# A hybrid encoder step on one core: key tiles of full height for the delta-rule state, one decay buffer, and closer transfers in the build-time plan

## The chip, the cores and the metric

The kernel runs on one core of a Trainium2 chip. A core has a matrix engine (TensorE, PE in the profile; PEld is its weight load), three elementwise engines (VectorE = DVE, ScalarE = ACT, GpSimd = POOL) and SyncE (SP), which issues nearly all transfers here. The engines run beside each other, each in the order of its own instruction list, and wait for each other by semaphores. Matmuls read SBUF and write PSUM, which has eight banks. The metric is device time of the core in microseconds; less is better.

## The reference, cut to what matters

Two layers over 2048 prompt frames and 32 frames of a running stream, width 1024, in float32. Layer 0 is sliding-window attention, layer 1 gated DeltaNet with 8 heads of 128 keys by 128 values, in chunks of 64 frames. Each layer has an input projection, a gate, an output projection and a residual add; RMSNorm stands ahead of each layer and at the end. The change concerns the delta rule, per head and chunk:

```
v_new = u - w @ s
o = (q * exp(g)) @ s + intra @ v_new
s = s * exp(g_last) + (k * exp(g_last - g)).T @ v_new
```

Here `u` and `w` come out of a triangular system in the chunk's keys, `s` is the 128x128 state of the head, and `intra` is the masked product of queries and keys times a decay.

## The kernel before, in words

The frames are cut into four slabs of 512 (the second carries the 32 sample frames too, 544 columns). All of layer 0 goes over the slabs, then all of layer 1. A projection is a run of blocks: 128 output features, 8 slices of the contraction, three matmuls each (the operands are split into a high and a low part in a faster float format), so 24 matmuls of 512 columns or 48 of 272 per block. In between, side work runs as generators: attention in layer 0, convolution and delta rule in layer 1.

In layer 1 the heads go in pairs: head x = 0 of a pair lives on partitions 0 to 63 (64 frames), head x = 1 on 64 to 127. Four chunks of a pair of heads are a *quad*, two quads a *pair* of a slab; with the sample's lone quad there are 33 quads, 132 chunks. Per quad, `local_quad` (line 1491) turns the keys from columns to frames through PSUM into `kd` (line 1507, 128 partitions by 4 chunks by 128), loads the decay table `e` (line 1502, two buffers), makes it an exponential, scales it, multiplies it with the products of keys and queries into `md`, `mo` and `it`, and scales `kd` (line 1546). `inverse` (line 1562) solves the triangular systems of both quads of a pair on VectorE, in some 62 dependent small steps with the tiles `tl` and `sub`, then transposes into `tq` (line 1597) and finishes with 32x32 matmuls. `chain_quad` (line 1635) goes through the chunks in order: state times keys and queries (`tb<-st,kq`), `r` on VectorE, the solve (`tb<-r,btt`; in the last pair the tile is called `kqs`), a copy `vn` on ScalarE, then the state's update and the output matmul (`tb<-vn,bit`), and on VectorE two state additions (`st`) and the output `o`. The update takes the two heads as two matmuls over 64 partitions each, into two PSUM tiles (`p3`, tag `tc`, and `p2`, tag `tb`). `p2` also holds the output matmul's result:

```
up = [p3[:, 0:P], p2[:, 2 * P : 3 * P]]
...
    self.mm(up[x], q["kd"][rows, c, :], vn[rows], True, True)
self.mm(p2[:, P : 2 * P], q["it"][:, c, :], vn, True, True)
```

A float32 matmul of the program shows as two passes in the profile.

The order on each engine is made at build time. Every operation is recorded with a cost (`Estimate`), and `Order.flush` (line 313) replays them as a list scheduler: on each engine the operation that can start first goes next; among those ready, the lowest rank, where an evacuation of a projection (`EVAC`) and the steps of the chain (`CHAIN`) are moved ahead. An operation on a PSUM bank waits for all earlier ones of other engines in that bank. Transfers are one queue in this plan: a transfer starts at the later of 1500 ns after its issue and the end of the one before it, lasts its bytes / 250 ns (line 150), and has landed 500 ns after that. Up to 25 us of plan time its length is taken times `CLOSE` = 0.7 (line 341). The plan has 216 ns for a projection matmul of 512 columns. The hardware keeps the order, not the times.

In layer 0, `out_blocks` (line 881) makes the output projection: each block loads the residual into `xr`, VectorE adds the product onto it (the evacuation), and the sum goes to memory. Weights arrive as `wr` and are split: ScalarE rounds to `wh` (high), VectorE subtracts to another `wh` (low); six `wh` buffers go round. Beside this, `keep_ahead` (line 425) loads the weights of layer 1, splits them and stores both parts, three transfers of 256 KB per half block.

Of the kernel before, what the change touches and what calls it, by code (L numbers as in the profile page):

```python
# [13 lines left out]
AF = mybir.ActivationFunctionType  # L14
ALU = mybir.AluOpType

P = 128
# [5 lines left out]
CH = 64  # L23
# [188 lines left out]
class Order:  # L212
# [2 lines left out]

    ENGINES = ("tensor", "vector", "scalar", "gpsimd", "sync")

    START, EARLY, CLOSE = 25000, 5000, 0.7

    EVAC, CHAIN = 400, 600  # L220
# [92 lines left out]
    def flush(self):  # L313

        overs = []
        for p in self.places.values():
            if p.old and p.over is None:
                p.over = Op(None)
                overs.append(p.over)
                for o in p.old.ops:  # L320
                    self.link(o, p.over)
                for o in {id(o): o for o in p.ops}.values():
                    self.link(p.over, o)
                    if o.gang:
                        self.link(p.over, o.gang)
        self.wait = {e: [] for e in self.ENGINES}
        ready = {e: [] for e in self.ENGINES}
        for o in [o for o in overs + self.ops if o.left == 0]:
            self.settle(o)
        while any(self.wait.values()) or any(ready.values()):  # L330
            when = {e: max(self.free[e], 0.0 if ready[e] else self.wait[e][0][0]) for e in self.ENGINES if ready[e] or self.wait[e]}
            e = min(when, key=when.get)
            now = when[e]
            while self.wait[e] and self.wait[e][0][0] <= now:
                _, rank, o = heapq.heappop(self.wait[e])
                heapq.heappush(ready[e], (rank, o))
            _, op = heapq.heappop(ready[e])
            op.call()
            if op.dma:
                self.free[e] = now + 60  # L340
                self.dma = max(now + 1500, self.dma) + op.cost * (self.CLOSE if now < self.START else 1)
                op.ends = {"dma": self.dma + 500}
            else:
                self.free[e] = now + op.cost
                op.ends = {e: self.free[e]}
            op.start = now
            self.finish(op)
        assert all(o.done for o in self.ops)
        self.ops = []
# [49 lines left out]
class Kern:  # L399
# [848 lines left out]
    def delta_setup(self, bp):  # L1248
        nc = self.nc
        self.bp = bp  # L1250
        one = lambda shape, tag, dt=F32: self.t(bp, shape, tag, dt, bufs=1)
        self.st = one([P, DNH, P], "st")
        self.hist = one([P, 24, 3], "hist")
        nc.gpsimd.memset(self.hist, 0.0)
        self.hsmp = one([P, 24, 3], "hsmp")
        nc.sync.dma_start(self.hsmp, self.io["cv"])
        self.csmp = one([P, 24, 3], "csmp")

        self.cw = one([P, 96], "cw")
        nc.vector.tensor_scalar(out=self.cw, in0=self.par[:, PC_CW : PC_CW + 96], scalar1=0.5, scalar2=None, op0=ALU.mult)  # L1260
        self.dg = one([P, 1], "dgn")
        nc.vector.tensor_scalar(out=self.dg, in0=self.par[:, PC_DG : PC_DG + 1], scalar1=0.5, scalar2=None, op0=ALU.mult)
        self.na_ = one([P, 4], "na")
        nc.scalar.activation(self.na_, self.par[:, PC_AL : PC_AL + 4], AF.Exp)
        nc.vector.tensor_scalar(out=self.na_, in0=self.na_, scalar1=-1.0, scalar2=None, op0=ALU.mult)

        self.tts = [one([P, 4, P], f"btt{i}") for i in range(2)]
        self.its = [one([P, 4, P], f"bit{i}") for i in range(4)]

        def zeros():  # L1270
            for x in (*self.its, *self.tts, self.st):
                nc.gpsimd.memset(x, 0.0)
                yield 1000

        self.spawn(zeros(), "zeros", 5000)
        self.npair = self.nconv = 0
        self.chained, self.order, self.quads, self.had = set(), [], [], [None, None]
# [213 lines left out]
    def local_quad(self, q, tab, off, md, mo, c0):  # L1491

        nc, bp, m = self.nc, self.bp, 4
# [5 lines left out]
        half = [slice(x * CH, (x + 1) * CH) for x in range(2)]  # L1499
        kq = q["kq"]  # L1500
        yield kq
        e = self.t(bp, [P, m, CH], "e", bufs=2)
        for x in range(2):
            src = tab["gcd"][x, off : off + m].rearrange("c t -> (c t)").unsqueeze(0).broadcast_to([CH, m * CH])
            nc.sync.dma_start(e[x * CH : (x + 1) * CH].rearrange("p c t -> p (c t)"), src)
        sx, ss = [self.t(bp, [P, 2, 4], k, bufs=b) for k, b in (("sx", 2), ("ss", 6))]
        kd = self.t(bp, [P, m, P], "kd", bufs=4)
        q["kd"] = kd
        for x, rows in enumerate(half):
            pk = yield from self.bank("ta")  # L1510
            for c in range(m):
                self.tp(pk[:, c * P : (c + 1) * P], kq[:, c, x, :])
            yield
            nc.scalar.copy(kd[rows].rearrange("p c d -> p (c d)"), pk[rows, : m * P])
            for c in range(m):
                junk = pk[:, c * P : (c + 1) * P]
                nc.scalar.activation(junk, junk, AF.Square, accum_out=sx[:, x, c : c + 1])
            self.give("ta")
            yield 0
# [20 lines left out]
        kds, ri, nbk = small("kds"), small("ri"), small("nbk")  # L1540
# [2 lines left out]
        nc.vector.scalar_tensor_tensor(out=nbk[:, :m], in0=ri[:, :m], scalar=-1.0, in1=tsl("egc"), op0=ALU.mult, op1=ALU.mult)  # L1543
        q["ri"], q["nbk"] = ri, nbk
        for c in range(m):
            nc.scalar.activation(kd[:, c, :], kd[:, c, :], AF.Copy, scale=kds[:, c : c + 1])
        yield e
        g = pg[:, : m * P].rearrange("p (c t) -> p c t", c=m)
        for x in range(2):
            rows = slice(x * CH, (x + 1) * CH)  # L1550
# [11 lines left out]
    def inverse(self, quads, md, mo):  # L1562


        nc, bp = self.nc, self.bp
        m = 4 * len(quads)
        cg, nj = 32 // m, m
# [26 lines left out]
            if j % 3 == 2:  # L1594
                yield

        tq = self.t(bp, [P, 8, 32], "tq", bufs=1)[:, :nj]
        nc.vector.transpose(out=tq, in_=t3.rearrange("p i j -> p j i"))
        tc_ = tq.rearrange("p j (g c) -> p c (j g)", g=cg)
        tr = self.t(bp, [P, 8, 32], "trc", bufs=1)[:, :m]  # L1600
# [34 lines left out]
    def chain_quad(self, q, tab, off, states, gated, put):  # L1635


        nc, bp, m = self.nc, self.bp, 4
        tt = nc.vector.tensor_tensor
        kq = q["kq"]  # L1640
# [5 lines left out]
        for c in range(m):  # L1646
            state = yield from states(c)
            p1 = yield from self.bank("tb")
            self.issue.lead = Order.CHAIN
            for x in range(2):  # L1650
                self.mm(p1[:, x * P : (x + 1) * P], kq[:, c, x, :], state[:, x, :], True, True)
            r = self.t(bp, [P, P], f"r{q['i']}", bufs=1)
            qs = self.t(bp, [P, P], f"qs{q['i']}", bufs=1)
            half = [slice(y * CH, (y + 1) * CH) for y in range(2)]
            for x, rows in enumerate(half):
                nc.vector.scalar_tensor_tensor(
                    out=r[rows], in0=p1[rows, x * P : (x + 1) * P], scalar=q["nbk"][rows, c : c + 1], in1=q["vb"][rows, c, :],
                    op0=ALU.mult, op1=ALU.add)
            for x, rows in enumerate(half[::-1]):
                nc.scalar.activation(  # L1660
                    qs[rows], p1[rows, x * P : (x + 1) * P], AF.Identity, scale=tab["egq"][rows, off + c : off + c + 1])
            self.give("tb")
            self.issue.lead = 0
            yield
            p2 = yield from self.bank("tb")
            self.issue.lead = Order.CHAIN
            self.mm(p2[:, 0:P], q["tt"][:, c, :], r, True, True)
            vn = self.t(bp, [P, P], f"vn{q['i']}", bufs=1)
            nc.scalar.copy(vn, p2[:, 0:P])
            self.issue.lead = 0  # L1670
            yield

            p3 = yield from self.bank("tc")
            up = [p3[:, 0:P], p2[:, 2 * P : 3 * P]]
            self.issue.lead = Order.CHAIN
            for x in range(2):
                rows = slice(x * CH, (x + 1) * CH)
                self.mm(up[x], q["kd"][rows, c, :], vn[rows], True, True)
            self.mm(p2[:, P : 2 * P], q["it"][:, c, :], vn, True, True)
            for x in range(2):  # L1680
                nc.vector.scalar_tensor_tensor(
                    out=state[:, x, :], in0=state[:, x, :], scalar=tab["egl"][:, x, off + c : off + c + 1],
                    in1=up[x], op0=ALU.mult, op1=ALU.add)
            tt(out=o[:, c, :], in0=p2[:, P : 2 * P], in1=qs, op=ALU.add)
            self.issue.lead = 0
            self.give("tb")
            self.give("tc")
            yield
            nc.scalar.activation(qs, o[:, c, :], AF.Square, accum_out=so[:, c : c + 1])
            states.done(c)  # L1690
# [562 lines left out]
```

## Time and profile before

| what | before |
|---|---|
| time, median of 3 runs | 2347.42 us (2346.01 to 2352.44) |
| profiled execution | 2349.7 us, of it span 2347.9 us |
| PE busy | 2243.8 us (96%), 14759 matmuls |
| DVE busy | 1724.0 us (73%) |
| ACT busy | 1262.7 us (54%) |
| POOL busy | 467.8 us (20%) |
| DMA | 382.75 MB, mean 163 GB/s |
| mean granted TensorE clock | 0.980 of full speed |

The span runs from the first to the last instruction; the time has a little around it. Busy is the union of an engine's instructions. Matmuls overlap each other in the records, so the distance from start to start tells what one costs in a row, not its length. Layer 1 begins at about 1000 us. All compute instructions carry the same source line (that of a recording helper), so groups are told apart by their tiles: `tc<-vn,kd` writes tile `tc` from `vn` and `kd`.

### The profile page before, as it was taken

To read this page: it belongs to the slowest core of one execution; us is meant where nothing else is said; L and a number is where in the kernel's file an instruction comes from. 1 tells how busy PE (TensorE), PEld (TensorE's weight loads), DVE (VectorE), ACT (ScalarE), POOL (GpSimd) and SP (SyncE) were. 2 spreads that over 40 slices of the span, in tenths; PEclk is the share of its full clock that TensorE was granted. 3 is DMA by queue.
4 is the path that set the end of the run, shared out by engine and by line. 5 is a ranking of instruction groups with operands and counts; after the bars stand their busy time and mean duration, and the time that the engine had idled before them with its cause. 6 is when DMAs were issued, how large, how long until landed. Compare 5 with 4: busy or idle time off the path is not lost.

```text
span 2347.9 us, 44428 instructions
## 1 busy us (share of the span) xinstructions
PE 2243.8 (96%) x14759; PEld 1842.6 (78%) x14759; DVE 1724.0 (73%) x5330; ACT 1262.7 (54%) x3792; POOL 467.8 (20%) x738
## 2 busy tenths in 40 slices
PE   8999999989999999999999999989999999999997
PEld 6777899877777777777788788867798777777776
DVE  7785667757665565688987677888886888786876
ACT  6664566546554553556566355465644465535533
POOL 0120000301110001222233031231313222122222
PEclk9999999999999999999999999999999999999998
DMA  8567655765443226544533673433457634476442
GB/s 272 190 203 231 219 187 183 222 220 193 153 138 112 66 64 203 180 133 127 173 95 112 207 240 102 133 115 125 149 177 226 188 117 137 139 225 206 153 139 68
DMA packets 222832, 382.75 MB, mean 163 GB/s; under 512 B 29922, under 2 KB 45194, under 8 KB 222602
## 3 DMA queue, kind: packets, MB, share of 16 engines
q1 hardware_dynamic: 220154, 377.75, 50.4%
q8 instruction: 116, 1.90, 0.3%
q10 hardware_dynamic: 2448, 2.16, 0.3%
q14 instruction: 114, 0.93, 0.1%
HBM read 311.63 MB, written 68.19 MB: 162 GB/s over the span
## 4 chain that ended last, share of the span: by engine, by line
PE 66%; DVE 22%; ACT 6%; issue 3%; DMA 1%; POOL 1%; SPq 0%; DVEq 0%; ACTq 0%; POOLq 0%
PE pj L185 47%; PE tb L185 7%; PE ta L185 6%; PE tc L185 4%; DVE cy L185 4%; DVE sub L185 3%; DVE tl L185 3%; ACT ta L185 2%; DVE ml L185 1%; DVE md L185 1%; DVE r L185 1%; PE ms L185 1%; ACT kd L185 1%; DVE st L185 1%; DVE kq L185 1%
## 5 line engine op out<-in xcount | busy, mean ns | idle before, releaser
L185 PE MATMUL pj<-hk,wh 128*128 128x512 f32 (+1 forms) x8184 | 1770.5, 363 | 34.0 <-DVE xr L185 16.3
L185 PEld LDWEIGHTS pj<-hk,wh 128*128 128x128 f32 x8184 | 1326.5, 191 | 246.4 <-issue 29.2
L185 DVE SCALAR_TENSOR_TENSOR cy<-cx,cw,cy 128x512 f32<-128x512 f32 x360 | 230.5, 651 | 45.7 <-ACT cy L185 40.9
L185 DVE TENSOR_TENSOR wh<-wr,wh 128x512 fp32r<-128x512 f32 x224 | 159.1, 712 | 139.5 <-ACT wh L185 129.4
L185 ACT CAST wh<-wr 128x512 fp32r<-128x512 f32 x224 | 138.0, 618 | 203.2 <-PE pj L185 174.0
L185 ACT ACTIVATE qs<-tb,egq 64x128 f32<-64x128 f32 x264 | 95.7, 362 | 90.5 <-DVE r L185 79.6
L185 POOL TENSOR_TENSOR hk<-of,hk 128x256 fp32r<-128x256 f32 (+1 forms) x72 | 53.4, 742 | 444.8 <-ACT hk L185 439.2
L185 ACT ACTIVATE s<-s,mx 128x256 f32<-128x256 f32 (+1 forms) x272 | 132.0, 487 | 7.5 <-DVE mx L185 7.2
L185 DVE TENSOR_TENSOR sub<-ml,tl 128x60 f32<-128x60 f32 (+24 forms) x527 | 125.8, 239 | 10.2
L185 ACT ACTIVATE cx<-cy 128x512 f32<-128x512 f32 (+1 forms) x96 | 61.1, 636 | 130.4 <-DVE cy L185 95.7
L185 DVE TENSOR_TENSOR tl<-tl,sub 128x60 f32<-128x60 f32 (+24 forms) x527 | 123.0, 233 | 10.1
L185 DVE CUSTOM_DVE_ANT_0 s<-ta,bias 128x256 f32<-128x256 f32 (+1 forms) x272 | 96.2, 404 | 25.6 <-PE ta L185 25.5
L185 DVE SCALAR_TENSOR_TENSOR r<-tb,nbk,vb 64x128 f32<-64x128 f32 x264 | 91.7, 348 | 29.8 <-PE tb L185 25.3
L185 ACT ACTIVATE qs<-o 128x128 f32<-128x128 f32 x132 | 40.7, 308 | 132.2 <-DVE o L185 126.8
L185 ACT COPY cx<-pj 128x512 f32<-128x512 f32 (+2 forms) x149 | 64.1, 445 | 77.8 <-PE pj L185 66.0
L185 PE MATMUL tb<-st,kq 128*128 128x128 f32 x512 | 95.0, 287 | 5.5 <-DVE st L185 5.0
L185 PEld LDWEIGHTS tb<-st,kq 128*128 128x128 f32 x512 | 82.7, 194 | 20.4 <-DVE st L185 12.3
L185 DVE SCALAR_TENSOR_TENSOR st<-st,egl,tc 128x128 f32<-128x128 f32 x128 | 44.3, 346 | 59.4 <-PE tc L185 56.9
L185 ACT COPY pt<-tb 128x512 f32<-128x512 f32 (+2 forms) x144 | 70.6, 528 | 26.4 <-PE tb L185 26.1
L185 DVE TENSOR_SCALAR s<-s,den 128x256 f32<-128x256 f32 (+1 forms) x272 | 81.7, 352 | 1.1
L185 PE MATMUL tc<-pt,vt 128*64 128x128 f32 (+2 forms) x1056 | 79.7, 279 | 1.1 <-DVE of L185 0.6
L185 POOL TENSOR_TENSOR so<-so,mhalf 128x4 f32<-128x4 f32 x33 | 36.8, 1114 | 216.4 <-DVE so L185 188.6
(242 smaller groups left out, 3447.8 us busy)
## 6 DMA issues: line engine op xcount, KB each, us to landing
wh<-xswwd SPq DMA_DIRECT2D x528, 256.0 KB, 2.9
wr<-in_wa SPq DMA_DIRECT2D x160, 256.0 KB, 3.3
wh<-xswwdo SPq DMA_DIRECT2D x112, 256.0 KB, 3.0
pr<-in_wd SPq DMA_DIRECT2D x66, 256.0 KB, 3.4
xswwd<-ph SPq DMA_DIRECT2D x66, 256.0 KB, 3.6
xswwd<-pr SPq DMA_DIRECT2D x66, 256.0 KB, 3.0
wr<-in_wao SPq DMA_DIRECT2D x64, 256.0 KB, 2.9
xa<-in_x SPq DMA_DIRECT2D x48, 256.0 KB, 4.0
```

The lines of the kernel that those rows point to most:

```text
L185: self.order.add(Op(self.name, lambda: call(*args, **kw), cost, op == "dma_start"), ins, outs)
```

## The change

The key tile becomes one of four fixed tiles, cleared once on POOL, of twice the width: each head has its own 128 columns per chunk, filled on its own 64 partitions, with zeros on the other 64. The state's update is then two matmuls over all 128 partitions, both into one PSUM tile. A quad takes its tile when the chain of the quad four before it is done. The decay table has one buffer instead of two, and `tq` shares the buffer of `sub`. In the plan, the factor 0.7 holds for every transfer.

```diff
-                self.dma = max(now + 1500, self.dma) + op.cost * (self.CLOSE if now < self.START else 1)
+                self.dma = max(now + 1500, self.dma) + op.cost * self.CLOSE
...
+        self.kds = [one([P, 4, 2, P], f"kd{i}") for i in range(4)]
...
-            for x in (*self.its, *self.tts, self.st):
+            for x in (*self.its, *self.kds, *self.tts, self.st):
...
-        e = self.t(bp, [P, m, CH], "e", bufs=2)
+        e = self.t(bp, [P, m, CH], "e", bufs=1)
...
-        kd = self.t(bp, [P, m, P], "kd", bufs=4)
-        q["kd"] = kd
+        while q["n"] >= 4 and "kq" not in self.quads[q["n"] - 4]["over"]:
+            yield 200
+        kd = q["kd"] = self.kds[q["n"] % 4]
...
-            nc.scalar.copy(kd[rows].rearrange("p c d -> p (c d)"), pk[rows, : m * P])
+            nc.scalar.copy(kd[rows, :, x, :], pk[rows, : m * P].rearrange("p (c d) -> p c d", c=m))
...
-            nc.scalar.activation(kd[:, c, :], kd[:, c, :], AF.Copy, scale=kds[:, c : c + 1])
+            both = kd[:, c].rearrange("p x d -> p (x d)")
+            nc.scalar.activation(both, both, AF.Copy, scale=kds[:, c : c + 1])
...
-        tq = self.t(bp, [P, 8, 32], "tq", bufs=1)[:, :nj]
+        tq = self.t(bp, [P, 32 * 8], "sub", bufs=1).rearrange("p (j i) -> p j i", i=32)[:, :nj]
...
-            up = [p3[:, 0:P], p2[:, 2 * P : 3 * P]]
+            up = [p3[:, x * P : (x + 1) * P] for x in range(2)]
...
-                rows = slice(x * CH, (x + 1) * CH)
-                self.mm(up[x], q["kd"][rows, c, :], vn[rows], True, True)
+                self.mm(up[x], q["kd"][:, c, x, :], vn, True, True)
```

## Rows read from the trace of the kernel before

**Rows 1.** Busy us (and instructions) by stretch, layer 1; clock, DMA share, GB/s.
```profile
core 0: us, PE busy (x) PEld busy (x) DVE busy (x) ACT busy (x) POOL busy (x), PEclk, DMA share, GB/s
1000.00:1400.00 400.00, 385.98 (x2696) 323.45 (x2695) 320.06 (x1035) 223.63 (x743) 106.14 (x184) 0.99 0.49 153
1400.00:1600.00 200.00, 180.94 (x1438) 161.00 (x1437) 165.93 (x553) 109.60 (x374) 51.87 (x107) 0.95 0.39 121
1600.00:1900.00 300.00, 293.87 (x1894) 241.14 (x1894) 238.21 (x747) 159.05 (x521) 71.64 (x119) 0.98 0.54 170
...
sum 1348.00, PE 1275.89 PEld 1051.90 DVE 1066.75 ACT 712.83 POOL 340.30; mean PE 255.18 PEld 210.38 DVE 213.35 ACT 142.57 POOL 68.06
```

**Rows 2.** Timeline of PE in two chunks: start us, us from first to last.
```profile
1499.93 0.61 PE L185 MATMUL tb<-st,kq 128*128 128x128 f32 x4
1500.30 5.96 PE L185 MATMUL pj<-hk,wh 128*128 128x272 f32 x45
...
1513.53 0.37 PE L185 MATMUL tc<-vn,kd 64*128 64x128 f32 x1
...
1513.95 0.49 PE L185 MATMUL tb<-vn,bit 128*128 128x128 f32 x2
1514.19 0.74 PE L185 MATMUL pj<-hk,wh 128*128 128x272 f32 x4
1514.77 0.38 PE L185 MATMUL tb<-st,kq 128*128 128x128 f32 x2
...
1516.61 1.00 PE L185 MATMUL pj<-hk,wh 128*128 128x272 f32 x6
1517.54 0.37 PE L185 MATMUL tc<-vn,kd 64*128 64x128 f32 x1
```

**Rows 3.** Groups by tiles and shape: busy us, mean ns | idle before.
```profile
L185 PE MATMUL tc<-vn,kd 64*128 64x128 f32 x264 | 65.3, 328 | 3.1 <-ACT vn L185 2.7
...
L185 ACT ACTIVATE kd<-kd,kds 128x128 f32<-128x128 f32 x132 | 43.0, 393 | 14.5 <-DVE kds L185 14.4
...
L185 ACT ACTIVATE hk<-hk,par 128x256 f32<-128x256 f32 x3 | 1.5, 499 | 0.0
```

**Rows 4.** Timeline of one chunk near the end, update to state additions.
```profile
2314.97 0.37 PE L185 MATMUL tc<-vn,kd 64*128 64x128 f32 x1
...
2315.39 0.49 PE L185 MATMUL tb<-vn,bit 128*128 128x128 f32 x2
2315.49 0.35 DVE L185 SCALAR_TENSOR_TENSOR st<-st,egl,tc 128x128 f32<-128x128 f32 x1 [1.13 <-PE tc L185]
...
2315.97 0.35 DVE L185 SCALAR_TENSOR_TENSOR st<-st,egl,tb 128x128 f32<-128x128 f32 x1
```

**Rows 5.** Instructions on tile `e`, last pair: ns min/median/max, first and last start.
```profile
L185 DVE TENSOR_TENSOR e<-e,gc x2: 414/414/415, 2192.8 to 2193.2; 128x256 f32<-128x256 f32 x2
...
L185 ACT ACTIVATE e<-e x2: 418/419/420, 2194.3 to 2195.1; 128x256 f32<-128x256 f32 x2
L185 POOL TENSOR_TENSOR e<-e,ss x2: 610/616/622, 2223.4 to 2233.7; 128x256 f32<-128x256 f32 x2
```

**Rows 6.** Tile `e` over the whole span: its 66 loads, issue to landing.
```profile
DMA to landing us min/median/max: 2.5/2.8/3.7
```

**Rows 7.** Timeline of DVE, last pair: end of the first quad's products.
```profile
2228.80 0.41 DVE L185 TENSOR_TENSOR bit<-ta,e 64x256 f32<-64x256 f32 x1
```

**Rows 8.** PE's waits, 222 to 256 and 460 to 505 us: total, times, longest.
```profile
PE pj L185 <- DVE xr L185: 6.9, 4, 1.9
...
PE pj L185 <- DVE xr L185: 9.0, 5, 1.8
```

**Rows 9.** Busy us by stretch, as in rows 1, for the same two stretches.
```profile
222.00:256.00 34.00, 26.62 (x138) 21.45 (x136) 14.63 (x31) 9.22 (x17) 0.00 (x0) 0.95 0.70 223
460.00:505.00 45.00, 36.02 (x247) 34.63 (x246) 19.11 (x33) 13.32 (x23) 0.00 (x0) 0.92 0.70 227
```

**Rows 10.** Timeline of DVE ahead of one such evacuation.
```profile
227.44 0.69 DVE L185 TENSOR_TENSOR wh<-wr,wh 128x512 fp32r<-128x512 f32 x1 [1.80 <-ACT wh L185]
228.05 0.68 DVE L185 TENSOR_TENSOR xr<-pj,xr 128x512 f32<-128x512 f32 x1
```

## The prediction, made before the changed kernel ran

> **What bounds the kernel now.** I read first the busy time by stretch. In the second layer, from 1000 us on, TensorE is busy 1275.89 of 1348 us, VectorE 1066.75 and ScalarE 712.83 [rows 1]. The reader is to see two things there: TensorE is the engine that runs out of time, and its idle time is uneven. In 700 us (1000 to 1400, 1600 to 1900) it is busy 97%; from 1400 to 1600 us it is busy 90% with VectorE at 83%, so there it waits for results. Work taken off TensorE is worth its full price in the first kind of stretch and less in the second. Then TensorE's own timeline inside one chunk of the delta rule, which prices the matmuls of the state update by their starts [rows 2]. For the ordering estimate, last, what TensorE waits for in the first layer: the evacuation of an output block by VectorE [rows 8], and what stands ahead of that evacuation [rows 10].
>
> **State update over full height: TensorE.** A chunk's update now is two matmuls over 64 rows each, in two passes (float32), the two heads beside each other in the two halves of the array. The first pair of passes starts at 1513.53, the next matmul (over `bit`, two passes) at 1513.95, the projection behind it at 1514.19 [rows 2]. So a pair takes 0.21 us. The 0.24 us of `bit` are one more such step and 0.03 us from the last pass to the projection. The group takes 0.66 us. Over full height it is six passes. The row at 1499.93 shows full-height passes of that size behind each other: four, with the projection 0.37 us after the first, which leaves (0.37 - 0.03) / 3 = 0.11 us a pass. Six passes: 5 x 0.11 + 0.03 = 0.58 us, 0.08 us less than now.
> The change of height has a price ahead of the group too. Projections of 272 columns follow each other at 5.96 us / 45 = 0.13 us. Four of them lead in 0.58 us to a full-height matmul (1514.19 to 1514.77); six should lead to one in 0.58 + 2 x 0.13 = 0.84 us, but to the half-height one they take 0.93 us (1516.61 to 1517.54) [rows 2]. So entering half height costs 0.09 us, which goes. Together 0.17 us a chunk; 264 passes of one head are 132 chunks [rows 3]: **23 us of TensorE time less**. If the price of entering stays, 0.08 x 132 = 11 us.
> A rule that speaks against this edit: the Trainium skill, TensorEngine Tiling, section Theoretical Speedup, has it that with a contraction of 64 rows or fewer two tiles side by side run up to twice as fast. By it a pair should cost one full-height pass, and the change would add two passes of 0.11 us to each chunk, 29 us in all. The row has 0.21 us for a pair, so here two halves side by side cost what two full passes cost.
> How much of the 23 us reaches the end? At full price in the 700 dense us (52% of the layer) and a third in the rest it is 0.52 + 0.16 = 0.68 of it; I take **-16 us** (bounds: -4, a third of the smaller price, and -23).
>
> **The state's read-back.** Both products now lie in one PSUM tile, the output matmul in another. Before, the second head's product shared its tile with the output matmul. Where VectorE was free, the first state addition began at 2315.49, 0.52 us after the update's first pass at 2314.97 (0.31 us after the second, by the step of 0.21), and the second only at 2315.97, behind the output matmul that began at 2315.39 [rows 4]. After: four passes, the last one beginning at 0.33 us, so the first addition at 0.64 us, less the 0.09 us of the earlier entry: 0.03 us later than now. The second addition can follow it without the wait for the output matmul, about 0.3 instead of 0.48 us behind. A chunk's chain gets some 0.15 us shorter. That counts where the chain alone sets the pace: the last 12 chunks, 12 x 0.15 = **-2 us** (bounds: +2, if the granted clock is low there and the four passes cost double, and -3).
>
> **Larger key tiles.** The scaling on ScalarE goes over 256 columns instead of 128: 393 ns now, 499 ns for a scaled 128x256 [rows 3], so 132 x 0.106 = 14 us more on an engine that is busy 713 of 1348 us. It hides beside projections; where the chunk's copy `vn` is queued behind one it comes 0.1 us later. I take **+1** (0 to +14). The four clearing memsets stand on POOL ahead of the layer's first key copy, while projections run: 0, and some us once if the first copy had to wait. The explicit wait before a tile is taken asks for the chain of the quad four back, which the start of the pair already asks for: 0. `tq` in the buffer of `sub` comes and goes in the order that VectorE has now, and its readers on TensorE end before `xs` is written anyway: 0.
>
> **One decay buffer instead of two.** Now both quads of a pair find `e` loaded and exponentiated long before: done by 2195.5 in the last pair, used from 2223.4 on [rows 5]. After, the second quad's load starts only when the first quad's last product with `e` is done. From there: load 2.8 us (2.5 to 3.7) [rows 6], then subtraction, mask and exponential, 1.9 us from 2192.8 to the end of the first exponential (2194.3 + 0.42), with some 0.1 us between, 4.8 us in all. In the last pair the first quad ends at 2228.80 + 0.41 [rows 7], so its partner's scaling of `e` can come at 2234.0; it came at 2233.7 [rows 5]. The last pair sets the end, so **+0.5** there (up to +3 if a step queues). In earlier pairs the inverse starts some us later, beside projections; I take **+0.5** for them and hold the other end as a rival. Behind the waiting load on SP stand the weight loads; but SP waits for the same event now, with the load of the quad after that, so nothing new is blocked.
>
> **The ordering estimate.** The plan gives a 256 KB transfer 262144 / 250 = 1049 ns on one queue; past 25 us of plan time the factor 0.7 (734 ns) was not used. In the first layer's output blocks about seven such transfers go out per block by the code: two of weights, the residual in, the sum out, and three of the kept copies. That is 7.3 us of the plan's queue against 24 projections x 0.216 = 5.2 us of its TensorE. So its queue falls behind, it believes that the residual lands late, and places the evacuation behind work that depends on the next slot of weights. The timeline shows that order: VectorE idles 1.80 us, subtracts the weights at 227.44, and evacuates only at 228.05 [rows 10]. TensorE waits nine times for this, 6.9 + 9.0 = 15.9 us [rows 8], in two stretches whose granted clock is 0.95 and 0.92 of full speed; that is 0.05 x 34 + 0.08 x 45 = 5 us more [rows 9]. With 0.7 the seven transfers take 5.1 us of plan and the evacuation can move ahead. Bounds: -21 if all goes; 0 if it turns into waits for weights, because the transfers already fill 0.70 of these 79 us, 55 us, beside 62.6 us of TensorE work: nearly full once the waits go. I take half, **-11 us**. Elsewhere the plan's order shifts without a direction that I can read; for that I give back **+2**, between -10 and +15.
>
> **Sum.** -16 - 2 + 1 + 0.5 + 0.5 - 11 + 2 = -25. The profiled execution took 2349.7 us (span 2347.9, 1.8 around it), 2.3 above the median of the runs, 2347.42. So 2324.7 for such an execution, and **2322** against the median.
>
> **Rivals** (against the median).
> *Waits take the gain; no change.* The second layer is held by VectorE's results and the output blocks by transfers: -6 from TensorE, 0 from the plan, +2: 2343 us. For it: the stretch from 1400 us with VectorE at 83%. Against: the 700 us with TensorE at 97%.
> *The second decay table is late; slower.* Place: between the two quads of each pair. The second quad can end no sooner than 4.8 us plus its products, some 7 us, behind the first. Where it would follow at once that is 7 us later than now, in the last pair 0; at 3.5 us on average (an estimate) 16 pairs start their inverse 56 us later in sum. If three quarters of it showed as idle TensorE: +42 - 26 = +16, 2363 us. It decides from 26 us on, 1.6 us a pair. Against: each inverse has projections beside it.
> *Packing pays after all; slower.* If a pair's 0.21 us hid some other wait and two halves did cost one pass, the update gets dearer by 2 x 0.11 x 132: +29 - 9 = 2367 us. (That is what the rule of TensorEngine Tiling in the Trainium skill would make of it.) Against: the step of 0.21 us throughout [rows 2, 4].
> *Everything goes; faster still.* -23 - 21 - 3 + 2 = -45: 2302 us.
> *The estimate doesn't do what it should.* If the evacuation stays behind the weights, -14 is left: 2333 us, inside the forecast's own range.
>
> **How the numbers follow.** Forecast 0.58, with its own range 2308 to 2338; no change 0.16; late table 0.11; packing 0.02; everything 0.13. A measurement of this kernel tells 0.3%, 7 us, from no change. Faster: 0.58 + 0.13 and a little of the no-change case, 0.73; slower: 0.11 + 0.02 and 0.01 of the no-change case, 0.14; same: the rest, 0.13. The range goes from 2303, which leaves out about half of "everything", to 2350, which leaves out the slower cases.
>
> **What would show it.** Right: passes 0.11 us apart from the first update matmul to the projection, 0.58 us in all, and no longer step ahead of them; TensorE's busy time in the second layer about 20 us less; the second state addition about 0.3 us behind the first; TensorE's waits for the `xr` evacuation under 8 us. Wrong: `bit` still 0.42 us after the first update matmul; idle TensorE in the second layer up by 15 us or more; waits for `wr` on ScalarE, or for `e` on VectorE, of several us each.

## The result, and the profile after

The changed kernel takes 2317.53 us (median of 4 runs, 2313.39 to 2323.11), the kernel before 2347.41: a ratio of 0.9863, 95% interval 0.984 to 0.9885. The forecast was 2322 us. The profiled execution took 2321.29 us, 28.4 less than that of before, where the sum had 25.

The first copy of keys from PSUM into `kd` marks the start of the delta rule and cuts the program in two. Group of that copy, kernel before; behind the colon min/median/max ns, then first and last start:

```profile
L185 ACT COPY kd<-ta x66: 562/580/596, 962.7 to 2228.7; 64x512 f32<-64x512 f32 x66
```

The same group after the change:

```profile
L185 ACT COPY kd<-ta x66: 566/580/586, 947.8 to 2191.0; 64x512 f32<-64x512 f32 x66
```

So 14.9 us were gained before this point, and 13.7 behind it. Up to this point the order of instructions is that of plan_only (below), which has the plan's factor alone, so the first part is the factor's. TensorE (columns as in [rows 1]) up to the first key copy, before:

```profile
0.00:962.70 962.70, 931.21 (x6063) 761.47 (x6064) 628.88 (x1883) 530.64 (x1381) 113.84 (x148) 0.99 0.55 179
```

and after:

```profile
0.00:947.80 947.80, 930.30 (x6063) 761.85 (x6064) 629.86 (x1882) 531.44 (x1380) 115.75 (x151) 0.99 0.56 182
```

Its idle time falls from 31.5 to 17.5 us; its busy time and its clock stay. This part is the estimate at work. PE's wait for the evacuation `xr`, whole span, after (total us, times, longest; before it was 16.3 us in ten waits, nine of them in [rows 8]):

```profile
PE pj L185 <- DVE xr L185: 1.3, 3, 0.7
```

Timeline of DVE in the block that [rows 10] show, after: the evacuation `xr` now goes ahead of the subtraction `wh`.

```profile
227.36 0.68 DVE L185 TENSOR_TENSOR xr<-pj,xr 128x512 f32<-128x512 f32 x1
227.96 0.68 DVE L185 TENSOR_TENSOR wh<-wr,wh 128x512 fp32r<-128x512 f32 x1
```

Busy us by stretch, after, in the output blocks (columns as in [rows 1]; the answer to [rows 9], the blocks begin earlier now):

```profile
216.00:250.00 34.00, 32.42 (x154) 27.07 (x153) 19.68 (x33) 13.95 (x24) 1.03 (x1) 0.97 0.94 312
447.00:493.00 46.00, 45.15 (x348) 44.11 (x347) 26.29 (x47) 19.12 (x32) 0.40 (x1) 1.00 0.95 306
```

TensorE is busy 95% and 98% there, 78% and 80% before, and the granted clock is 0.97 and 1.00 of full speed. The transfers fill 0.94 and 0.95 of their engines' time, 0.70 before.

Behind the first key copy, whole stretch to the end, before:

```profile
962.70:2347.90 1385.20, 1312.59 (x8698) 1081.11 (x8696) 1095.11 (x3447) 732.10 (x2412) 353.93 (x590) 0.97 0.48 152
```

and after:

```profile
947.80:2319.30 1371.50, 1297.75 (x8699) 1096.18 (x8696) 1075.91 (x3448) 746.31 (x2413) 361.26 (x591) 0.98 0.49 154
```

TensorE's busy time is 14.8 us less and its idle time (72.6, now 73.8) the same. Part of that goes with the granted clock: by the clock records of the traces, TensorE stood at the lower of its two levels (1.2 GHz instead of 2.4) for 82 us of this stretch before and for 64 after. A projection of 272 columns follows the one ahead of it by 0.227 us at the lower level and by 0.125 at the higher (medians of the kernel before), so 18 us less of it are worth up to 8 us. The update itself looks as forecast where it lies between projections. Timeline of one late chunk after the change (the answer to [rows 4]):

```profile
2270.18 0.61 PE L185 MATMUL tc<-vn,kd 128*128 128x128 f32 x4
...
2270.63 0.39 PE L185 MATMUL tb<-vn,bit 128*128 128x128 f32 x2
...
2270.77 0.94 PE L185 MATMUL pj<-hk,wh 128*128 128x512 f32 x3
2270.83 0.61 DVE L185 SCALAR_TENSOR_TENSOR st<-st,egl,tc 128x128 f32<-128x128 f32 x2 [0.90 <-PE tc L185]
```

The group from first pass to projection is 0.59 us (forecast 0.58). Both state additions run as one pair, 0.65 us behind the first pass (forecast 0.64); two in 0.61 us at 0.35 us each [rows 4] puts the second 0.26 us behind the first.

The second decay table is late, as feared. VectorE's waits, after, whole span:

```profile
DVE e L185 <- DMA e<-xsgc: 16.7, 14, 2.2
```

### The profile page after: what moved, and what is told of

It reads as the page before. It is cut to its first block, busy times and chain, and to the rows that moved or that the text cites. A ratio compares the mean times of both kernels' runs of the same rounds, so it can differ in the third digit from the quotient of the medians.

```text
span 2319.3 us, 44386 instructions
## 1 busy us (share of the span) xinstructions
PE 2228.1 (96%) x14759; PEld 1858.0 (80%) x14759; DVE 1705.8 (74%) x5330; ACT 1277.8 (55%) x3792; POOL 477.0 (21%) x742
## 4 chain that ended last, share of the span: by engine, by line
PE 66%; DVE 18%; DMA 6%; ACT 5%; issue 3%; POOL 1%; SPq 0%; DVEq 0%; ACTq 0%; POOLq 0%
PE pj L185 49%; PE ta L185 7%; PE tb L185 6%; PE tc L185 4%; DVE cy L185 3%; DVE sub L185 2%; DVE tl L185 1%; DVE r L185 1%; DMA e<-xsgc 1%; ACT ta L185 1%; DVE ml L185 1%; DVE md L185 1%; DVE st L185 1%; PE ms L185 1%; DVE xa L185 1%
## 5 line engine op out<-in xcount | busy, mean ns | idle before, releaser
L185 PE MATMUL pj<-hk,wh 128*128 128x512 f32 (+1 forms) x8184 | 1743.6, 362 | 19.1 <-DMA wh<-xswwd 5.5
L185 DVE SCALAR_TENSOR_TENSOR cy<-cx,cw,cy 128x512 f32<-128x512 f32 (+1 forms) x360 | 234.6, 658 | 36.8 <-ACT cy L185 32.1
L185 DVE SCALAR_TENSOR_TENSOR st<-st,egl,tc 128x128 f32<-128x128 f32 x256 | 77.3, 343 | 56.2 <-PE tc L185 53.4
L185 ACT COPY cx<-pj 128x512 f32<-128x512 f32 (+3 forms) x149 | 63.9, 445 | 87.9 <-PE pj L185 64.4
L185 PE MATMUL tb<-st,kq 128*128 128x128 f32 x512 | 88.4, 289 | 12.8 <-DVE st L185 11.7
L185 PEld LDWEIGHTS tb<-st,kq 128*128 128x128 f32 x512 | 76.1, 193 | 30.1 <-DVE st L185 22.0
L185 PE MATMUL tc<-vn,kd 128*128 128x128 f32 x528 | 87.2, 288 | 3.4 <-ACT vn L185 2.7
L185 PEld LDWEIGHTS tc<-vn,kd 128*128 128x128 f32 x528 | 73.6, 194 | 20.7 <-ACT vn L185 16.3
L185 DVE TENSOR_TENSOR pr<-pr,ph 128x512 fp32r<-128x512 f32 x82 | 58.0, 707 | 36.9 <-ACT ph L185 30.5
```

The costliest lines, as they stand in the source:

```text
L185: self.order.add(Op(self.name, lambda: call(*args, **kw), cost, op == "dma_start"), ins, outs)
```

## The experiments

Each ratio is against the kernel before on the same chip. The runs lie on several chips, so kernels are compared by their ratios. The table has every one; a gain in us is (1 - ratio) x 2350.

| kernel | median us | ratio, 95% interval | gain us |
|---|---|---|---|
| the change | 2317.53 | 0.9863 (0.984 to 0.9885) | 32 |
| plan_only | 2325.54 | 0.9895 (0.9878 to 0.9912) | 25 |
| tiles_only | 2348.54 | 0.9984 (0.9972 to 0.9996) | 4 |
| after_oldbanks | 2329.56 | 0.991 (0.9892 to 0.9928) | 21 |
| after_e2 | 2310.2 | 0.9831 (0.9816 to 0.9847) | 40 |
| e2_oldbanks | 2319.77 | 0.9877 (0.9852 to 0.9903) | 29 |
| e2_half | 2325.8 | 0.9905 (0.9881 to 0.993) | 22 |
| banks_fixed | 2310.04 | 0.9835 (0.9813 to 0.9857) | 39 |
| banks_fixed_half | 2319.86 | 0.9875 (0.9854 to 0.9896) | 29 |
| plan_e1 | 2351.87 | 1.0001 (0.9987 to 1.0016) | 0 |
| plan_e1_order | 2350.73 | 1.0006 (0.9991 to 1.0021) | -1 |
| e2_pj | 2380.94 | 1.0132 (1.0108 to 1.0156) | -31 |
| e2_close75 | 2302.4 | 0.9798 (0.9776 to 0.982) | 47 |

**The two halves of the change, each alone.** plan_only is the kernel before with this edit; tiles_only is the changed kernel without it:

```diff
-                self.dma = max(now + 1500, self.dma) + op.cost * (self.CLOSE if now < self.START else 1)
+                self.dma = max(now + 1500, self.dma) + op.cost * self.CLOSE
```

> The kernel before with the factor 0.7 on every transfer of the plan, nothing else. Theory (two separate gains, one per layer): -13 us against the kernel before (-8 to -18), all of it in layer 0: the first key copy, 962.7 us before, comes near 948; TensorE's waits for the xr evacuation fall from 16.3 us to under 3; layer 1 takes as long as before, within 5 us. Rival (the plan gives it all, the tiles nothing): -28 us, and layer 1 is 10 us or more shorter too.

> The changed kernel with the old rule of the plan (factor 0.7 only in the first 25 us). Theory: -15 us against the kernel before (-10 to -22), none of it before the first key copy at 962.7 us (within 2 us); waits for xr stay at 16 us. Rival (the plan gives it all): within 7 us of the kernel before. Rival (the two need each other): less than 8 us gain here and in the plan alone.

The plan alone gains 25 us, the tiles alone 4. That is nearer to the rival by which the plan gives it all than to the theory; what the tiles are worth beside the factor is taken up with the height below. PE's wait for `xr` in plan_only:

```profile
PE pj L185 <- DVE xr L185: 0.4, 1, 0.4
```

and in tiles_only:

```profile
PE pj L185 <- DVE xr L185: 16.7, 11, 1.9
```

So the factor removes these waits. The first key copy starts at 949.9 us in plan_only, 12.8 us earlier than before, and at 965.3 in tiles_only, 2.6 later. With the factor, that point lies between 943.6 and 953.0 in all kernels but one (e2_pj, whose plan differs in its projection prices too). That is 10 to 19 us of gain in the first layer, about 14; kernels with one order there differ by several us, so a single profile says no more.

But plan_only gains as much again behind that point, where its instructions are those of before and only their order is new. Whole stretch from the first key copy on, plan_only:

```profile
949.90:2322.30 1372.40, 1306.18 (x8698) 1073.66 (x8696) 1087.74 (x3447) 731.14 (x2412) 356.50 (x590) 0.98 0.49 153
```

1372.4 us against 1385.2, half of it less busy TensorE and half less idle. No term of the forecast has this. The instructions being the same, the busy half can be the clock's: 65 us at the lower level against 82. And tiles_only, which was to have 15 us, has 4: behind the first key copy its TensorE is busy 11.4 us less than before, but idle 8.3 us more.

**One edit undone at a time.** after_e2 gives the decay table its second buffer back (for room, a small tile shares the buffer of `tl`); after_oldbanks puts the second product back beside the output matmul:

```diff
-        e = self.t(bp, [P, m, CH], "e", bufs=1)
+        e = self.t(bp, [P, m, CH], "e", bufs=2)
-        tr = self.t(bp, [P, 8, 32], "trc", bufs=1)[:, :m]
+        tr = self.t(bp, [P, 32 * 8], "tl", bufs=1).rearrange("p (c t) -> p c t", t=32)[:, :m]
```

```diff
-            up = [p3[:, x * P : (x + 1) * P] for x in range(2)]
+            up = [p3[:, 0:P], p2[:, 2 * P : 3 * P]]
```

> The changed kernel with two decay buffers again; to make room, trc takes the buffer of tl, which is dead by then. Theory (one buffer delays every second quad, and a little of that reaches the end): second quads scale e right behind the first as before, time -32 to -36 us against the kernel before, that is 2 to 6 us below the changed kernel. Rival (the delay is hidden): -30, within 3 us of the changed kernel. If the one buffer cost what the slower rival said, more than 10 us below it.

> The changed kernel with the second head's product back in the tile of the output matmul (full height kept). Theory: TensorE's steps unchanged (0.58 us from the first update pass to the projection), the second state addition again 0.45 us or more behind the first where VectorE is free, time +1 to +4 us against the changed kernel (-26 to -29 against the kernel before). Rival (the read-back gains nothing): within 1 us of the changed kernel. Both lie near what can be told; the spacing of the additions decides.

Read at face value, one buffer costs 7.5 us and the banks are worth 11, where the expectations had 2 to 6 and 1 to 4 (the intervals of the change and of after_e2 overlap). e2_oldbanks, with both edits, has the second number again, 0.9877 against 0.9831:

> Two decay buffers (as in after_e2), full height, but the second head's product in the tile of the output matmul. Theory (buffer and PSUM tile each cost their own): after_oldbanks was 21 us below the kernel before and the buffer is worth 8, so -29 us (-25 to -33). Rival (the order of the plan makes the differences, no part has a price of its own): anywhere from -21 to -41, with layer 0 as in after_e2.

For the first number, plan_e1 is plan_only with `bufs=1` for `e`:

> The kernel before with the factor 0.7 on every transfer and one decay buffer; key tiles as before. Theory (one buffer costs about 8 us by itself, since every pair's second quad gets its table late): -17 us against the kernel before, 8 us above plan_only, all in layer 1. Rival (it costs only beside the large tiles or by chance of the order): within 3 us of plan_only (-25).

It loses all of plan_only's 25 us. The theory that the buffer costs some 8 us by itself, whatever the order, fell with it. Since each of these edits also hands the planner another problem, the order had to be held still.

**The same order, one thing changed.** In plan_e1_order the plan believes in one buffer and makes plan_e1's order; the program has two. In banks_fixed the plan believes in the new bank and makes after_e2's order; the second product really goes to the old one:

```diff
-    def t(self, pool, shape, tag, dt=F32, bufs=1):
-        x = pool.tile(shape, dt, tag=tag, bufs=bufs, name=self.nm(tag))
+    def t(self, pool, shape, tag, dt=F32, bufs=1, real=None):
+        x = pool.tile(shape, dt, tag=tag, bufs=real or bufs, name=self.nm(tag))
...
-        e = self.t(bp, [P, m, CH], "e", bufs=1)
+        e = self.t(bp, [P, m, CH], "e", bufs=1, real=2)
```

```diff
+            self.issue.swap = {id(up[1]): (up[1], p2[:, 2 * P : 3 * P])}
...
+            self.issue.swap = {}
```

(`swap` replaces the operand when the instruction is issued, after it was recorded.)

> plan_e1 (which lost all 25 us that plan_only had gained) with two real decay buffers but planned as if there were one: the order of every engine is that of plan_e1, only the wait of the second table for the first is gone. Theory (the plan's order is what costs, as the banks showed): within 6 us of plan_e1, that is 0 to -6 us against the kernel before. Rival (the wait itself costs, tables come late for every second quad): near plan_only, -19 to -25.

> after_e2 with the second head's product in the tile of the output matmul, but planned as if it were not: the order of every engine is that of after_e2, only the wait of the second state addition for the output matmul is added. Theory (the wait lengthens every chunk's chain by 0.15 to 0.2 us, which counts only where the chain sets the pace): 2 to 4 us slower than after_e2, about -37 us against the kernel before. Rival (the wait itself costs what after_oldbanks lost): 9 to 13 us slower, -29. Rival (the loss of after_oldbanks was its order): within 1 us of after_e2.

Neither wait has a price that shows in the order where it was tried. For the buffer this says less than it seems. 1.0006 against 1.0001: the second buffer gives nothing back in plan_e1's order, but that order has the lateness written into it. The load no longer waits for the first quad's last product with its table, yet VectorE and POOL take up the second table where a plan with one buffer put it. In one pair of quads of plan_e1_order, that product and then the scaling of the second table:

```profile
1029.18 0.41 DVE L185 TENSOR_TENSOR bit<-ta,e 64x256 f32<-64x256 f32 x1
1035.19 0.61 POOL L185 TENSOR_TENSOR e<-e,ss 128x256 f32<-128x256 f32 x1 [1.14 <-ACT e L185]
```

and in the same pair of plan_only, where the scaling comes first:

```profile
1026.19 0.61 POOL L185 TENSOR_TENSOR e<-e,ss 128x256 f32<-128x256 f32 x1
1030.08 0.42 DVE L185 TENSOR_TENSOR bit<-ta,e 64x256 f32<-64x256 f32 x1
```

Counted over the 16 pairs, the scaling starts 6.4 us behind the end of that product in plan_e1 and 6.1 behind it in plan_e1_order (medians), in plan_only 0.7 us ahead of it; in the changed kernel it is 6.3 us behind, in after_e2 0.5 ahead. So the test takes the wait away and keeps the late use. What the lateness itself costs stays open.

0.9835 against 0.9831: in after_e2's order the old bank costs nothing that shows. The intervals leave some 6 us either way, which shuts out the 9 to 13 us of the rival, but not the theory's 2 to 4. The second state addition does come later in part of the chunks. In banks_fixed, timeline of one of them:

```profile
2267.63 0.30 PEld L187 LDWEIGHTS tc<-vn,kd 128*128 128x128 f32 x2 [0.46 <-ACT vn L187]
2267.64 0.49 PE L187 MATMUL tc<-vn,kd 128*128 128x128 f32 x2 [0.22 <-ACT vn L187]
...
2267.96 0.39 PE L187 MATMUL tb<-vn,kd 128*128 128x128 f32 x2
...
2268.16 0.35 DVE L187 SCALAR_TENSOR_TENSOR st<-st,egl,tc 128x128 f32<-128x128 f32 x1
2268.18 0.39 PE L187 MATMUL tb<-vn,bit 128*128 128x128 f32 x2
...
2268.66 0.35 DVE L187 SCALAR_TENSOR_TENSOR st<-st,egl,tb 128x128 f32<-128x128 f32 x1 [0.16 <-ACT hk L187]
```

0.50 us between the two additions, against 0.26 in the changed kernel. They are 0.45 us or more apart in 46 of 128 chunks; the median is 0.26 us in banks_fixed and in after_e2. So most of the 11 us of the banks come out of the order that the plan makes of its beliefs. For the 7.5 and the 25 us of the buffer that is not shown apart from the lateness.

How plan_e1's order loses shows in part in one wait. TensorE's wait for the output tile `o` before its transposes, from the first key copy on, in plan_e1:

```profile
PE ta L185 <- ACT o L185: 14.5, 7, 4.5
```

and in plan_only:

```profile
PE ta L185 <- ACT o L185: 3.3, 4, 2.1
```

**The height, at the same order.** e2_half is e2_oldbanks and banks_fixed_half is banks_fixed with the update over 64 rows again; every engine has the same instructions in the same order, but for the height of these:

```diff
-                self.mm(up[x], q["kd"][:, c, x, :], vn, True, True)
+                self.mm(up[x], q["kd"][x * CH : (x + 1) * CH, c, x, :], vn[x * CH : (x + 1) * CH], True, True)
```

> e2_oldbanks with one edit: the update's matmuls take their own 64 rows of the same tiles, so half height again; the order of every engine is the same, instruction by instruction. Theory (height saves 0.17 us of TensorE a chunk, 23 us, two thirds of it open): 16 us slower than e2_oldbanks (10 to 23), that is about -13 us against the kernel before. Rival (TensorE waits anyway, the saving is lost in its waits): within 4 us of e2_oldbanks. Rival (packing pays): faster than e2_oldbanks.

> banks_fixed (which ran 1.65% below the kernel before, -39 us) with the update's matmuls on their own 64 rows: half height at the same order of every engine, a second pair of kernels for the price of the height. Theory A (0.17 us of TensorE a chunk, 23 us, two thirds open): 16 us slower than banks_fixed, -23 against the kernel before. Theory B (as the pair e2_half and e2_oldbanks gave, the saving is mostly lost in TensorE's waits): 3 to 10 us slower, -29 to -36. Rival (the height is worth nothing): within 3 us.

Half height is slower by 6.6 us in the first pair (0.9905 against 0.9877) and by 9.4 in the second (0.9875 against 0.9835). The intervals overlap in both pairs, in the second by a hair; together they say about 8 us, half of the 16 expected (the second is in the range of its theory B). The granted clock, median of the runs, is 0.9865 and 0.987 of full speed in the first pair and 0.987 and 0.984 in the second, so part of the second's 9.4 us may be the clock. What the price is made of can be read in two chunks that both stand behind three projections. TensorE at half height, banks_fixed_half:

```profile
2275.74 0.93 PE L187 MATMUL pj<-hk,wh 128*128 128x512 f32 x3
2276.60 0.37 PE L187 MATMUL tc<-vn,kd 64*128 64x128 f32 x1
2276.61 0.37 PE L187 MATMUL tb<-vn,kd 64*128 64x128 f32 x1
2276.81 0.27 PE L187 MATMUL tc<-vn,kd 64*128 64x128 f32 x1
2276.82 0.27 PE L187 MATMUL tb<-vn,kd 64*128 64x128 f32 x1
2277.02 0.49 PE L187 MATMUL tb<-vn,bit 128*128 128x128 f32 x2
2277.26 1.41 PE L187 MATMUL pj<-hk,wh 128*128 128x512 f32 x5
```

and at full height, banks_fixed:

```profile
2262.62 0.93 PE L187 MATMUL pj<-hk,wh 128*128 128x512 f32 x3
2263.39 0.38 PE L187 MATMUL tc<-vn,kd 128*128 128x128 f32 x2
2263.61 0.39 PE L187 MATMUL tb<-vn,kd 128*128 128x128 f32 x2
2263.83 0.39 PE L187 MATMUL tb<-vn,bit 128*128 128x128 f32 x2
2263.97 1.41 PE L187 MATMUL pj<-hk,wh 128*128 128x512 f32 x5
```

0.86 + 0.66 us against 0.77 + 0.58: 0.09 us for entering and 0.08 for the group, 0.17 together, the forecast's two prices to the hundredth. The two chunks are typical: counted over the records at the higher clock level, the median from the start of a 512-column projection to the first pass is 0.326 us at half height and 0.234 at full, and from there to the projection behind the group 0.666 and 0.589. The stretch from the first key copy to the end, banks_fixed_half:

```profile
950.60:2318.10 1367.50, 1304.16 (x8698) 1071.20 (x8696) 1094.93 (x3447) 748.47 (x2412) 359.30 (x590) 0.98 0.49 154
```

and banks_fixed:

```profile
943.60:2303.40 1359.80, 1289.85 (x8698) 1088.65 (x8696) 1094.73 (x3447) 745.26 (x2412) 359.24 (x590) 0.98 0.49 155
```

TensorE is busy 14.3 us longer at half height, not 23. In the other pair, e2_half:

```profile
951.70:2321.40 1369.70, 1298.03 (x8698) 1063.17 (x8696) 1085.49 (x3447) 746.66 (x2412) 353.79 (x590) 0.99 0.49 154
```

and e2_oldbanks:

```profile
953.00:2330.40 1377.40, 1294.23 (x8698) 1091.84 (x8696) 1085.07 (x3447) 745.26 (x2412) 355.71 (x590) 0.98 0.48 153
```

it is only 3.8 us longer. But there the half-height execution stood at the lower clock level for 33 us of the stretch and the other for 56; in the pair above it is 60 and 55. With 0.45 of the time at the lower level taken off (0.125 against 0.227 us a projection), the pairs say about 12 and 14 us, an estimate.

The 0.17 us hold where the chunk follows projections closely. Where the group starts right behind the copy `vn`, as in the chunk of banks_fixed at 2267.64 shown above, the weights are loaded only from 2267.63 on, and the first full-height pass takes 0.21 us before the next (0.32 from the first to the third, against 0.22 at 2263.39). At half height the step is 0.21 in either case. In banks_fixed 50 of 133 groups have such a longer first step (0.15 us or more), counted over the records: at 0.1 us that is some 5 us. Of these 50, 47 start within 0.11 us of the end of `vn`; the 83 others all start 0.12 us or more behind it. Some 20 groups do not stand behind a projection, where the entry was priced. And of the 14.3 us, 6.6 come back as idle TensorE (1367.50 - 1304.16 = 63.3 us at half height, 1359.80 - 1289.85 = 70.0 at full).

**Can the order be made better on purpose?** Two tries on after_e2: e2_pj gives the plan a projection price fitted to the trace (233 and 124 ns for 512 and 272 columns, the plan had 216 and 116), and e2_close75 sets `CLOSE` to 0.75.

```diff
-                return max(107.0, n / 2.4) + 3
+                return max(107.0, n / 2.2)
```

```diff
-    START, EARLY, CLOSE = 25000, 5000, 0.7
+    START, EARLY, CLOSE = 25000, 5000, 0.75
```

(`n` is the number of columns.)

> after_e2 with the plan's price of a projection matmul set to what the trace shows (233 ns instead of 216 for 512 columns, 124 instead of 116 for 272). Theory (a plan nearer to the chip gives a better order): 3 to 15 us below after_e2, -43 to -55 against the kernel before. Rival (a change of the plan's prices deals a new order at random): anywhere within 12 us of after_e2, either way.

> after_e2 with the factor 0.75 instead of 0.7 on the plan's transfers. Theory (what counts is that the plan's transfer queue no longer falls behind; 0.75 does that too): layer 0 within 5 us of after_e2 and no xr waits there; layer 1 differs by the luck of the order, up to 10 us either way. Rival (0.7 is the point): layer 0 loses half of its 14 us.

The truer price makes the kernel 1.3% slower than before and 71 us slower than after_e2, far outside the rival's 12 us too; that a plan nearer to the chip gives a better order is refuted in this one try. Its first key copy starts at 965.1 us, as late as before, though its waits for `xr` are gone (1.7 us), and the rest takes 1413.2 us, 28 more than before. The factor 0.75 gives the lowest median of all, 2302.4 us. That is below both kernels (the interval ends at 0.982, that of the change begins at 0.984), but its interval touches those of after_e2 and banks_fixed. I have no reading of why, other than the order.

## Why the prediction was right, and where not

**The time.** 2322 forecast, 2317.53 measured. The two halves of the sum fit too: -11 for the first layer against 14.9 in the profile, -14 for the rest against 13.7. The second fit is partly luck, as its terms show.

**The ordering estimate: mechanism right, size low.** The evacuation moved ahead of the weights and nine or ten waits went, as foreseen. I halved the 21 us for fear of full transfers. They did get nearly full (0.95), but among TensorE's waits ahead of the first key copy there is none for a transfer. Of the 15.9 us of waits 14 came off TensorE's idle time; the 5 us for the clock did not come, as its busy time there is 931.2 us before and 930.3 after. The term was -11 and should have been about -14.

**Full height: price right, reach too high.** The price per chunk was right, and packing lost to full passes as the rows of before said. The rule of the Trainium skill (TensorEngine Tiling, Theoretical Speedup) would make half height 29 us cheaper on TensorE; at equal order the traces have it some 12 to 14 us dearer. But -16 was to reach the end and about 8 do. Two steps failed: that all 132 chunks pay the full 0.17 us (12 to 14 us in all, not 23), and that 0.68 of it gets through (8 of these, by medians with wide intervals).

**The read-back.** Its step is as forecast (0.26 us between the additions, forecast 0.3), its worth was to be -2. As a wait, in after_e2's order, it is worth nothing that shows; through the order it moved 11 us.

**The decay buffer.** The lateness came in full. In the median of the pairs the second table is scaled 6.3 us behind the first quad's last product (4.8 forecast), where with two buffers (after_e2) it is 0.5 us ahead, and VectorE waited for it 14 times, 16.7 us. The rival (2363) put it at 3.5 us on average, so its lateness was right and more; but three quarters of that was to show as idle TensorE, and 16 pairs of 7 us cost 7.5 us here. My +1 was too low by some 6 us, if the 7.5 are the buffer's. In plan_e1 the same lateness goes with 25 us, and what else its order does is open. I had also said that nothing new is blocked behind the load on SP: behind the first key copy TensorE waits for weights 6.8 us in the changed kernel and 1.2 in after_e2, and no run shows whether they stood behind the table.

**The larger key tiles** and the shared buffers were not measured by themselves. The scaling takes 498 ns (499 forecast). e2_half has them without the height and the bank, and is about 2 us slower than plan_only (0.9905 against 0.9895), which the intervals don't tell from nothing.

**Order shifts: the step that was mis-sized.** I gave them +2, between -10 and +15. The bank moved the time by 11 us through the order, the buffer with its lateness by 7.5 and 25, and prices in the plan alone by -25, -8 and +71 us (plan_only against before, e2_close75 and e2_pj against after_e2). Of the 30 to 32 us, the first layer's 14 and the height's 8 are the part with a mechanism shown. The other 8 to 10 us are the net of orders, a bank's gain and a buffer's loss among them. The granted clock moves with the orders, and the forecast had it in the first layer only: the median over the runs is 0.979 of full speed before, 0.982 in plan_only, 0.9855 after and 0.974 in e2_pj. Over 50 runs of the kernel before, 0.01 of clock goes with 14 us, so by this estimate some 9 of the 32 us go with the clock. No run shows whether an order gains because it keeps the clock up or keeps the clock up because it waits less. Why the second layer's order in plan_only is 13 us better than before stays open too: half of it lies in many waits and half in TensorE's busy time, with the clock, and no run took one decision of the plan out of it.

## What to carry to other kernels

Where a list scheduler makes the order at build time, an edit's own price (here 0 to 14 us) can be smaller than what the new order does (here up to 71 us): put the known mechanism and a wide term for the order into the forecast, and test an edit by holding the order still and changing only what the chip sees. Look whether the order that is held was itself made around the effect, as plan_e1's was around the late table, and compare the clock before the busy time. For these float32 updates of 128 columns, two half-height matmuls side by side were no saving over full height with zeros; look at the step from start to start, before and behind the group. And an edit that only helps when something else is placed well (tiles_only, 4 us) should not be priced by its instructions.

## What the hardware showed that I had not expected

The transfers ran at 0.94 to 0.95 of 16 engines' time, 306 to 312 GB/s, in the output blocks of the first layer, while TensorE was busy 95 to 98%: nearly full transfers did not hold up the matmuls there. And a full-height pass that starts within 0.11 us of the end of the copy that it reads takes 0.21 us instead of 0.11 until the next one, so the cheaper form gains least just where the chain is waited for.
